# Even mixer: the division by the softmax sums on VectorE, and new tick counts for the normalised keys and the rotated queries

## The chip, the cores and the metric

The kernel runs on one core of one Trainium2 chip. The time is that of one execution on the device, in microseconds (us), and the median over the runs is compared. Engines are named as the profile names them: PE is TensorE's matmuls, PEld its weight loads, DVE is VectorE, ACT is ScalarE, POOL is GpSimd, SP is SyncE, whose queue issues the weight loads from HBM.

## The reference

A trunk of two layers on 256 tokens of width 1024, all in float32. Each layer is: half a SwiGLU block, a mixer, half a SwiGLU block. The mixer of layer 0, the "even" mixer, is the one the change touches:

```python
def even_mixer(h, w_in, q_gain, k_gain, sink, w_out, rope1, rope_axial):
    proj = h @ w_in                      # 1024 -> qa, ka, va, qb, kb, vb
    ...
    qa = apply_axial_rope(rms_norm(qa, q_gain), *rope_axial)   # 8 heads of 64
    ka = apply_axial_rope(rms_norm(ka, k_gain), *rope_axial)   # 2 key heads
    oa = global_gqa(qa, ka, va)
    qb = apply_rope(qb, *rope1)                                # 8 heads, plain
    kb = apply_rope(kb, *rope1)                                # 2 key heads
    ob = windowed_gqa_sink(qb, kb, vb, sink)
    return jnp.concatenate([oa, ob], axis=-1) @ w_out

# in both attentions
    p = jnp.exp(s - m)
    denom = jnp.sum(p, axis=-1)          # group b: + exp(sink - m)
    p = p / denom
    o = p @ v
```

Group "a" has normalised queries and keys and attends to all tokens; group "b" has plain ones, a window of 128 and a sink logit for each head. Layer 1 has another mixer ("odd"), which the change leaves alone.

## The kernel before

**Tiling.** Tokens are two tiles of 128 (`tt` 0 and 1). Weights come as pieces of 128 x 512. Each piece is split on the chip into a high part (`hi`, ACT, line 319) and the rest (`lo`, DVE, line 322), and each product takes three matmuls of 128x128 by 128x512: hi·hi, lo·hi and hi·lo (lines 311, 312, 313). Such a group of three is called a *triple* below. `th` and `tl` are the two parts of the transposed activations. Three of the eight PSUM banks are for keys' projections and attention scores (`s`), two for projections (`pj`), two for transposes (`tp`), one for attention outputs (`o`).

**Order.** PE, ACT, DVE and SP each execute their instructions in the order in which the program emits them. That order is set by *ticks*: each triple ends with one tick, and a tick steps every task (a Python generator) whose count has run out. `yield n` in a task means "go on n ticks later". So a number such as `ROPE_WAIT` is no time, but a count of triples that are emitted in between. A tick also may supply the next weight piece (`hi` at once, `lo` at the next tick). If nothing can be multiplied, ticks pass without a triple and the tasks' instructions stand close together.

**The even mixer's steps.** First the keys and values of both groups are projected (one bank `s` for each `tt`), then the queries of b, then those of a (banks `pj`). Four tasks `keys(g, tt)` evict, rotate (POOL, `rope`, lines 700 and 717), transpose on PE (`kr`, line 764) and split into `kT..z` (ACT) and `kT..x` (DVE, and a POOL copy, line 424). For group a they also normalise, by squares on ACT, a sum on DVE (`ssq`, line 728), a power on POOL (line 331) and a multiplication on POOL (line 759). Four tasks `queries(g, tt)` rotate on DVE (`t`, lines 700 and 702, `qr`, line 715), transpose on PE (line 394) and split into `qT..`, ACT's half and then DVE's.

The attention walks through group b, then group a, and in each through `tt`, then two pairs of heads (`b0`), then two halves `s`: eight *steps* for each group, numbered 1 to 8 below. A step is: scores on PE (lines 624, 625, and the mask, 628), maxima on DVE (`m`, 637), for b the sink (POOL, `es`, 573), exponentials with sums on ACT (`p`, 666; `es`, 577), `tot` and the reciprocal `r` on DVE (675, 678), the multiplication of `p` by `r` (680), four transposes on PE (688), their copy on ACT (`pt`, 584); after each second step the product with the values (`o`, 609) and its split `oT..h`, `oT..l`. A new step's scores start a fixed number of ticks after those before. The first step of a `tt` starts when the task of its queries has ended (`has_q`). Then `out_proj` multiplies by the output weights, for group b while group a's attention runs, then for group a, and adds to `x` (line 446).

The tick counts that the change touches stand at the top of the file:

```python
ROPE_WAIT = 3
KB_WAIT = 6
KA_WAITS = [2, 5]
```

Of the kernel before, what the change touches and what calls it, by code (L numbers as in the profile page):

```python
# [40 lines left out]
R_WAIT = 3  # L41
GLU_WAIT = 5
NAT_WAIT = 2
ROPE_WAIT = 3
KB_WAIT = 6
KA_WAITS = [2, 5]
QA_WAIT = 9
EVEN_GAP = {'a': 2, 'b': 2}
ODD_GAP = [4, 3]
# [73 lines left out]
class Trunk:  # L123
# [76 lines left out]
    def plan(self):  # L200
# [49 lines left out]

        yield from ffn("ffn1", 0, 0)
        yield from even()
        yield from ffn("ffn2", 0, 2)
        yield from ffn("ffn1", 1, 3)
# [476 lines left out]
    def even(self, sink):  # L731
        nc = self.nc
        self.rate = EVEN_RATE
        flat = lambda t: t.rearrange("p a b -> p (a b)")
        tab = {
            "a": [[self.gtab[:, tt, i, :] for i in range(4)] for tt in range(NT)],
            "b": [[self.tab[:, tt, i, :] for i in (4, 5, 2, 3)] for tt in range(NT)],
        }
        axial = {"a": 2, "b": 1}
        kT = {g: self.keys_tiles([P, T], f"kT{g}") for g in "ab"}  # L740
        vv = {g: [self.t([P, P], f"v{g}{tt}") for tt in range(NT)] for g in "ab"}
        qT = {g: [[], []] for g in "ab"}
        oT = {g: [[], []] for g in "ab"}
        by = [None, None]
        made = {"a": [], "b": []}

        def keys(g, tt, ps):
            yield 1
            r = self.rstd_of(tt)
            o = 256 if g == "b" else 0  # L750
            k = self.t([P, 2, HD], f"k{g}", 2)
            kr = self.t([P, 2, HD], f"kr{g}", 2)
            nc.scalar.activation(flat(k), ps[:, o : o + P], AF.Copy, scale=r)
            nc.scalar.activation(vv[g][tt], ps[:, o + P : o + 2 * P], AF.Copy, scale=r)
            if g == "a":
                sq = self.squares(k, 2, 1.0)
                yield KA_WAITS[0]
                n = self.head_rstd(sq, 2)
                nc.gpsimd.tensor_tensor(k, k, n.unsqueeze(2).to_broadcast([P, 2, HD]), op=ALU.mult)
                yield KA_WAITS[1]  # L760
            self.rope(nc.gpsimd, kr, k, 2, axial[g], *tab[g][tt][2:])
            yield KB_WAIT
            tb = self.bank("tp")
            nc.tensor.transpose(tb[:, :P], flat(kr), self.ident)
            yield 1
            at = slice(tt * P, tt * P + P)
            yield from self.stack_k(tb[:, :P], *([t[:, at] for t in tiles] for tiles in kT[g]))

        def queries(g, tt, ps):
            yield 1  # L770
            r = self.now.r[tt]
            x = ps.rearrange("p (a b) -> p a b", a=8)
            qr = self.t([P, 4, 2, HD], "qr", 2)
            if g == "a":

                sq = self.squares(x, 8, r)
                self.rope(nc.vector, qr, x, 8, axial[g], *tab[g][tt][:2])
                yield QA_WAIT
                n = self.head_rstd(sq, 8)
                by[tt] = self.little([P, 8], f"by{tt}")  # L780
                nc.gpsimd.tensor_scalar(by[tt], n, r, 1.0, op0=ALU.mult, op1=ALU.mult)
            else:
                self.rope(nc.vector, qr, x, 8, axial[g], *tab[g][tt][:2], r)
                yield ROPE_WAIT
            tb = self.turned(qr.rearrange("p j s d -> p (j s d)"))
            yield 1
            yield from self.stack_q(tb, f"qT{g}{tt}", 1, qT[g][tt])

        def heads(g):
            return self.attend(  # L790
                lambda tt: qT[g][tt],
                lambda tt: len(made[g]) > 2 + tt and all(task[1] is None for task in made[g][: 3 + tt]),
                lambda b: kT[g],
                lambda b, s, kc: vv[g][kc][:, s * HD : s * HD + HD],
                lambda: True,
                f"oT{g}",
                oT[g],
                EVEN_GAP[g],
                EVEN_WAITS[g],
                nc.gpsimd,  # L800
                sink=sink if g == "b" else None,
                scale=(lambda tt, b, s: by[tt][:, s * 4 + b : s * 4 + b + 2]) if g == "a" else None,
            )

        def both():
            yield from heads("b")
            yield from heads("a")


        W = self.take(KD)  # L810
        for tt in range(NT):
            ps = self.project(self.ready(tt), W, "s")
            for g in "ba":
                made[g].append(self.start(keys(g, tt, ps)))
        attention = None
        for g in "ba":
            W = self.take(KD)
            for tt in range(NT):
                ps = self.project(self.now.hT[tt], W, "pj")
                made[g].append(self.start(queries(g, tt, ps)))  # L820
                if attention is None:
                    attention = self.start(both())
        self.out_proj([oT["b"], oT["a"]], attention)
# [261 lines left out]
```

## Time and profile before

| what | before |
|---|---|
| median of 3 runs | 979.89 us (979.39 to 980.45) |
| the profiled execution's own time | 978.92 us |
| its span, first to last instruction | 977.1 us |
| PE busy | 965.5 us (99%) |
| DVE busy | 607.7 us (62%) |
| ACT busy | 546.0 us (56%) |
| POOL busy | 85.7 us (9%) |
| granted TensorE clock | 0.998 |

The even mixer takes about 200 us to 287 us of the span. Read the shares of the whole span with care: they average over blocks that have nothing in common. In the SwiGLU blocks PE runs without a gap; what the change can move is in the mixer, and there the row to look at is the idle time of PE and the instruction that ended it. A matmul's end is modelled, so the starts of consecutive matmuls tell more than the busy time.

### The profile page before, as it was taken

The page shows a single profiled execution, that of the slowest core. Times are in us where ns is not written, and L with a number is a line of the kernel's source. Part 1 is how long each engine was busy: PE and PEld are TensorE (multiplying, and loading weights), DVE is VectorE, ACT ScalarE, POOL GpSimd, SP SyncE. Part 2 cuts the span into 40 slices and gives each one's busy share as a digit, 9 for nine tenths or more (in the row PEclk, how much of TensorE's full clock was granted, in tenths as well). Part 3 has the DMA queues.
Part 4 walks back from the last instruction along what each step waited for, and adds up shares of the span by engine and source line. Part 5 has one row for each costly group of instructions (what it writes and reads, how often), then busy time and mean ns, then how long its engine had stood idle before and what let it go on. Part 6 is the DMA issues. An engine that isn't in the chain of part 4 may idle for free.

```text
span 977.1 us, 13724 instructions
## 1 busy us (share of the span) xinstructions
PE 965.5 (99%) x4908; PEld 818.6 (84%) x4908; DVE 607.7 (62%) x1195; ACT 546.0 (56%) x1152; POOL 85.7 (9%) x152
## 2 busy tenths in 40 slices
PE   9999999999999999999999999999999999999997
PEld 6888998877788889988888899888888888889886
DVE  6565575488866555654655566548879675555643
ACT  7544564477786544544644446447777664545430
POOL 0020000063420000000000000101331000000002
PEclk9999999999999999999999999999999999999999
DMA  8665576554226555766456456646545355547621
GB/s 290 223 205 172 182 251 214 168 135 120 96 91 208 176 157 158 246 215 197 148 176 197 145 173 231 223 153 197 181 128 170 130 172 181 186 131 235 237 87 43
DMA packets 82373, 171.70 MB, mean 176 GB/s; under 512 B 3712, under 2 KB 25216, under 8 KB 82304
## 3 DMA queue, kind: packets, MB, share of 16 engines
q1 hardware_dynamic: 81728, 170.23, 54.0%
q8 instruction: 38, 0.62, 0.3%
q10 hardware_dynamic: 576, 0.59, 0.2%
q14 instruction: 31, 0.25, 0.1%
HBM read 169.76 MB, written 1.05 MB: 175 GB/s over the span
## 4 chain that ended last, share of the span: by engine, by line
PE 95%; DVE 2%; ACT 1%; POOL 1%; issue 1%; DMA 0%; POOLq 0%; ACTq 0%
PE pj L311 14%; PE pj L313 14%; PE pj L312 14%; PE s L313 13%; PE s L312 13%; PE s L311 13%; PE tp L394 2%; PE o L311 2%; PE o L312 2%; PE o L313 2%; PE o L609 2%; PE tp L688 1%; PE tp L366 1%; PE s L624 1%; PE s L625 1%; DVE lo L322 1%
## 5 line engine op out<-in xcount | busy, mean ns | idle before, releaser
L322 DVE TENSOR_TENSOR lo<-raw,hi 128x512 fp32r<-128x512 f32 (+1 forms) x664 | 423.2, 671 | 239.1 <-ACT hi L319 235.0
L319 ACT ACTIVATE hi<-raw 128x512 fp32r<-128x512 f32 (+1 forms) x664 | 371.9, 606 | 169.4 <-PE s L313 102.4
L311 PE MATMUL pj<-hi,th 128*128 128x512 f32 (+1 forms) x512 | 197.8, 386 | 0.0
L313 PE MATMUL pj<-hi,tl 128*128 128x512 f32 (+1 forms) x512 | 192.8, 377 | 0.0
L312 PE MATMUL pj<-lo,th 128*128 128x512 f32 (+1 forms) x512 | 192.5, 376 | 0.0
L311 PE MATMUL s<-hi,th 128*128 128x512 f32 (+1 forms) x400 | 152.1, 380 | 0.0
L313 PE MATMUL s<-hi,tl 128*128 128x512 f32 (+1 forms) x400 | 149.2, 373 | 0.0
L312 PE MATMUL s<-lo,th 128*128 128x512 f32 (+1 forms) x400 | 148.9, 372 | 0.0
L313 PEld LDWEIGHTS pj<-hi,tl 128*128 128x128 f32 x512 | 96.1, 188 | 15.5
L311 PEld LDWEIGHTS pj<-hi,th 128*128 128x128 f32 x512 | 96.4, 188 | 13.0 <-issue 0.3
L312 PEld LDWEIGHTS pj<-lo,th 128*128 128x128 f32 x512 | 96.4, 188 | 12.8
L319 ACT ACTIVATE g_h<-tp 128x512 fp32r<-128x512 f32 (+1 forms) x48 | 27.0, 563 | 126.4 <-PE tp L394 126.4
L313 PEld LDWEIGHTS s<-hi,tl 128*128 128x128 f32 x400 | 75.2, 188 | 11.2
L312 PEld LDWEIGHTS s<-lo,th 128*128 128x128 f32 x400 | 75.3, 188 | 10.5 <-DVE lo L322 0.2
L311 PEld LDWEIGHTS s<-hi,th 128*128 128x128 f32 x400 | 75.3, 188 | 10.1
L313 PE MATMUL s<-hi,g_l 128*128 128x512 f32 (+2 forms) x198 | 73.6, 372 | 0.0
L312 PE MATMUL s<-lo,g_h 128*128 128x512 f32 (+2 forms) x198 | 73.5, 371 | 0.0
L311 PE MATMUL s<-hi,g_h 128*128 128x512 f32 (+2 forms) x198 | 73.5, 371 | 0.0
L505 DVE SCALAR_TENSOR_TENSOR glu<-pj,rstd,silu 128x512 f32<-128x512 f32 (+1 forms) x48 | 33.7, 702 | 45.1 <-PE pj L313 45.1
L500 ACT ACTIVATE silu<-s,rstd 128x512 f32<-128x512 f32 (+1 forms) x48 | 31.4, 654 | 51.1 <-PE s L313 50.6
L331 POOL TENSOR_TENSOR rstd<-var,mhalf 128x1 f32<-128x1 f32 (+2 forms) x16 | 12.9, 808 | 375.8 <-DVE var L329 375.8
L322 DVE TENSOR_TENSOR g_l<-tp,g_h 128x512 fp32r<-128x512 f32 (+1 forms) x48 | 30.8, 642 | 23.1 <-ACT g_h L319 23.1
(245 smaller groups left out, 1133.7 us busy)
## 6 DMA issues: line engine op xcount, KB each, us to landing
raw<-in_ffn_w_down SPq DMA_DIRECT2D x44, 1024.0 KB, 5.0
raw<-in_ffn_w_up SPq DMA_DIRECT2D x32, 1024.0 KB, 5.2
raw<-in_ffn_w_gate SPq DMA_DIRECT2D x30, 1024.0 KB, 5.1
raw<-in_ffn_w_gate SPq DMA_DIRECT2D x16, 768.0 KB, 4.4
raw<-in_ffn_w_up SPq DMA_DIRECT2D x16, 768.0 KB, 4.4
raw<-in_odd_w_qkv SPq DMA_DIRECT2D x12, 1024.0 KB, 5.2
raw<-in_even_w_in SPq DMA_DIRECT2D x4, 1024.0 KB, 5.1
raw<-in_even_w_out SPq DMA_DIRECT2D x8, 512.0 KB, 5.7
```

Source lines behind the costliest of these rows:

```text
L311: mm(ps, h, wh, start=first, stop=False)
L312: mm(ps, h, wl, start=False, stop=False)
L313: mm(ps, l, wh, start=False, stop=last)
L319: self.nc.scalar.activation(hi, src, AF.Copy)
L322: self.nc.vector.tensor_tensor(lo, src, hi.bitcast(F32), op=ALU.subtract)
L331: nc.gpsimd.tensor_tensor(r[:, :n], v[:, :n], self.mhalf[:, :n], op=ALU.pow)
L366: nc.tensor.transpose(tb[:, j * P : (j + 1) * P], self.x[tt][:, b * P : (b + 1) * P], self.ident)
L394: self.nc.tensor.transpose(tb[:, i * P : (i + 1) * P], src[:, i * P : (i + 1) * P], self.ident)
L500: nc.scalar.activation(s[:, :w], g[:, :w], AF.Silu, scale=self.rstd_of(tt))
L505: nc.vector.scalar_tensor_tensor(m[:, :w], u[:, :w], self.now.r[tt], s[:, :w], op0=ALU.mult, op1=ALU.mult)
L609: self.nc.tensor.matmul(O[64 * s : 64 * s + 64, i * P : i * P + P], v(b0 + i, s, kc), pT[s][:, i, kc, :], start=(kc == 0), stop=(kc == 1),)
L624: nc.tensor.matmul(S[:, i, :], q, kz[s], start=True, stop=False)
```

## The change

Four edits in the even mixer. The multiplication of the exponentials by the reciprocal sums (line 680) goes from POOL to DVE for both groups. The tasks of the normalised keys (group a) wait 8 ticks instead of 2 before their sum of squares, 4 instead of 5 before the rotation, and 10 instead of 6 before the transpose; the plain keys keep 6. The transposes of b's rotated queries come after 5 ticks instead of 3. And each query task ends two ticks later, so that the first scores of its `tt` can start only then.

```diff
-ROPE_WAIT = 3
-KB_WAIT = 6
-KA_WAITS = [2, 5]
+ROPE_WAIT = 5
+KB_WAIT = {'a': 10, 'b': 6}
+KA_WAITS = [8, 4]
...
-            yield KB_WAIT
+            yield KB_WAIT[g]
             tb = self.bank("tp")
             nc.tensor.transpose(tb[:, :P], flat(kr), self.ident)
...
             tb = self.turned(qr.rearrange("p j s d -> p (j s d)"))
             yield 1
             yield from self.stack_q(tb, f"qT{g}{tt}", 1, qT[g][tt])
+
+            yield 2
...
                 EVEN_GAP[g],
                 EVEN_WAITS[g],
-                nc.gpsimd,
+                nc.vector,
                 sink=sink if g == "b" else None,
```

How instructions move is shown at three places. In the listings a name carries the number of its buffer, and these numbers differ between the two kernels.

**Place 1, ACT, when group b's attention starts.** `qTb` from `tp_2474` (before) or `tp_2451` (after) is the split of b's second query tile; `p_2440` and `p_2465` are the exponentials of step 1, `p_2464` and `p_2493` those of step 2, and the table load stands ahead of the first exponential. Before:

```order
L319 ACTIVATE hi_2404<-raw_1891 128x512
L666 ACT_TABLE_LOAD
L666 ACTIVATE p_2440,sums_2367<-s_2369,m_637_2401 128x256 x2
L577 ACTIVATE es_2368<-es_2368 128x2
L319 ACTIVATE hi_2450<-raw_1891 128x512
L666 ACTIVATE p_2464,sums_2367<-s_2392,m_642_2414 128x256 x2
L577 ACTIVATE es_2368<-es_2368 128x2
L319 ACTIVATE qTb_662_2492<-tp_2474 64x512
L319 ACTIVATE qTb_663_2493<-tp_2474 64x512
```

After:

```order
L319 ACTIVATE hi_2435<-raw_1959 128x512
L319 ACTIVATE qTb_655_2461<-tp_2451 64x512
L319 ACTIVATE qTb_656_2462<-tp_2451 64x512
L666 ACT_TABLE_LOAD
L666 ACTIVATE p_2465,sums_2394<-s_2396,m_644_2422 128x256 x2
L577 ACTIVATE es_2395<-es_2395 128x2
L319 ACTIVATE hi_2475<-raw_1959 128x512
L319 ACTIVATE kTaz_524_2030<-tp_2459 64x128
L319 ACTIVATE kTaz_525_2031<-tp_2459 64x128
```

The split of the second query tile stood behind the exponentials of steps 1 and 2, and now stands ahead of the table load and of both. On PE its transposes (`tp_2451`) stand right behind the scores of step 3, one triple and the transpose of the second normalised key (`tp_2459`) follow, and after one more triple come the scores of step 4.

**Place 2, DVE, near the end of group b's attention.** `pj_2569` (before) and `pj_2508` (after) are a's second query tile, whose rotation is `t` and `qr`; `sums_2628` and `sums_2650` belong to steps 7 and 8. Before:

```order
L675 TENSOR_TENSOR tot_2736<-sums_2628,es_2629 128x2
L678 RECIPROCAL r_2738<-tot_2736 128x2
L675 TENSOR_TENSOR tot_2760<-sums_2628,es_2629 128x2
L678 RECIPROCAL r_2762<-tot_2760 128x2
L700 TENSOR_TENSOR t_8_741_2769<-pj_2569,gtab 128x512
L700 TENSOR_TENSOR t_8_742_2770<-pj_2569,gtab 128x8x16 x4
L715 TENSOR_TENSOR qr_2766<-t_8_741_2769,t_8_742_2770 128x4x64 x2
```

After:

```order
L700 TENSOR_TENSOR t_8_728_2720<-pj_2508,gtab 128x512
L700 TENSOR_TENSOR t_8_729_2721<-pj_2508,gtab 128x8x16 x4
L715 TENSOR_TENSOR qr_2717<-t_8_728_2720,t_8_729_2721 128x4x64 x2
...
L322 TENSOR_TENSOR qTa_740_2763<-tp_2745,qTa_740_2763 64x512
L322 TENSOR_TENSOR qTa_741_2764<-tp_2745,qTa_741_2764 64x512
L675 TENSOR_TENSOR tot_2789<-sums_2650,es_2651 128x2
L678 RECIPROCAL r_2791<-tot_2789 128x2
L680 TENSOR_SCALAR p_2785<-p_2785,r_2791 128x256 x2
L675 TENSOR_TENSOR tot_2811<-sums_2650,es_2651 128x2
L678 RECIPROCAL r_2813<-tot_2811 128x2
```

The reciprocals of steps 7 and 8 stood ahead of that rotation; now they stand behind it, behind the split of a's first query tile and, in the rows left out, behind two `lo`, `oTb02l`, the sums `ssq` and the maxima of step 8.

**Place 3, DVE, when group a's attention starts.** `qTa` here is the split of a's second query tile, and `s_2869`, `s_2887`, `s_2924` (before) and `s_2905`, `s_2922`, `s_2949` (after) are the scores of a's steps 1, 2, 3. Before:

```order
L637 TENSOR_REDUCE m_2905<-s_2869 128x2
L652 TENSOR_TENSOR m_781_2907<-m_2905,by_748_2791 128x2
L637 TENSOR_REDUCE m_2916<-s_2887 128x2
L652 TENSOR_TENSOR m_785_2918<-m_2916,by_748_2791 128x2
L322 TENSOR_TENSOR qTa_782_2912<-tp_2900,qTa_782_2912 64x512
L322 TENSOR_TENSOR qTa_783_2913<-tp_2900,qTa_783_2913 64x512
L322 TENSOR_TENSOR lo_2932<-raw_2184,hi_2931 128x512
L678 RECIPROCAL r_2941<-sums_2868 128x2
L678 RECIPROCAL r_2956<-sums_2868 128x2
L637 TENSOR_REDUCE m_2960<-s_2924 128x2
```

After:

```order
L322 TENSOR_TENSOR qTa_778_2897<-tp_2885,qTa_778_2897 64x512
L322 TENSOR_TENSOR lo_2913<-raw_2177,hi_2912 128x512
L637 TENSOR_REDUCE m_2927<-s_2905 128x2
...
L678 RECIPROCAL r_2963<-sums_2904 128x2
L680 TENSOR_SCALAR p_2960<-p_2960,r_2963 128x256 x2
L446 SCALAR_TENSOR_TENSOR x_86<-pj_2856,x_86 128x512
L678 RECIPROCAL r_2976<-sums_2904 128x2
L680 TENSOR_SCALAR p_2973<-p_2973,r_2976 128x256 x2
L637 TENSOR_REDUCE m_2980<-s_2949 128x2
```

The maxima of steps 1 and 2 stood ahead of the split of the second query tile and now stand behind it; between the reciprocals and the maxima of step 3 there are now two pairs of multiplications and an addition to `x`. On PE four triples that stood between the scores of a's steps 1 to 5 now stand earlier, and the scores of steps 3, 4 and 5 follow each other without a triple.

## The prediction

> **What bounds the kernel now.** I read the page first, then the idle time of PE by releaser, then PE, DVE and ACT in order of time through the mixer, last the share of each engine by stretch.
>
> ```profile
> PE 965.5 (99%) x4908; PEld 818.6 (84%) x4908; DVE 607.7 (62%) x1195; ACT 546.0 (56%) x1152; POOL 85.7 (9%) x152
> 220.00:230.00 10.00, 9.55 (x56) 7.76 (x56) 9.46 (x25) 7.00 (x19) 3.77 (x10) 1.00 0.56 128
> 250.00:260.00 10.00, 9.98 (x64) 8.07 (x63) 9.63 (x21) 4.76 (x10) 3.57 (x3) 1.00 0.33 108
> 260.00:270.00 10.00, 9.94 (x68) 7.79 (x67) 8.66 (x21) 8.96 (x28) 4.07 (x10) 1.00 0.34 105
> ```
>
> The first line is the span: PE bounds it, and DVE at 62% looks free. The others are stretches of the mixer; behind the length come PE, PEld, DVE, ACT and POOL. There DVE is busy 87 to 96%, nearly as long as PE. What is put on DVE here has little room, whatever the page's average says.
>
> ```profile
> 210.93 0.39 PE L312 MATMUL pj<-lo,th 128*128 128x512 f32 x1
> 211.16 0.39 PE L313 MATMUL pj<-hi,tl 128*128 128x512 f32 x1
> 212.40 0.33 PE L764 MATMUL tp<-mats,kra 128*128 128x128 f32 x1 [0.85 <-POOL kra L717]
> 217.37 0.63 PE L394 MATMUL tp<-mats,qr 128*128 128x128 f32 x4 [0.34 <-DVE qr L715]
> 220.18 0.39 PE L624 MATMUL s<-kTbz,qTb 128*128 128x256 f32 x1 [0.70 <-DVE qTb L322]
> ...
> 230.56 0.63 PE L688 MATMUL tp<-mats,p 128*128 128x128 f32 x4 [0.83 <-ACT pt L584]
> ...
> 249.40 0.47 PE L311 MATMUL pj<-hi,oTb00h 128*128 128x512 f32 x1 [0.75 <-DVE t L700]
> ```
>
> Start, duration, what, and in brackets PE's idle time and what ended it. Matmuls start 0.23 us apart (a triple is 0.69), so after 211.16 the next could start at 211.39 and started at 212.40: an idle time of 0.85 stands for 1.01 lost, 0.16 more than shown. So the five waits lose 1.01, 0.50, 0.86, 0.99 and about 0.9. They are what the mixer can give back, 4.3 us or 0.4%.
>
> **The change part by part.** *Normalised keys later.* Their rotation on POOL leaves the path of the plain keys, and their transposes stand 14 triples later: the wait at 212.40 goes. *Transposes of queries, and first scores, later.* Five ticks cover the rotation and four more triples stand ahead of the first scores, so the waits at 217.37 and 220.18 go. Together 2.37 gained. POOL has its chain done: before, the second plain key waited there behind the first normalised one; SP's loads keep their order. What is late next is worked out along the chain.
>
> *Step A, to the transposes of b's second query tile.*
>
> ```profile
> 223.18 1.28 ACT L666 ACT_TABLE_LOAD   x1 [2.04 <-DVE m L659]
> 224.47 0.47 ACT L666 ACTIVATE p<-s,m 128x256 f32<-128x256 f32 x1
> 225.39 0.20 ACT L577 ACTIVATE es<-es 128x2 f32<-128x2 f32 x1
> 226.63 0.28 PE L624 MATMUL s<-kTbz,qTb 128*128 128x256 f32 x1
> 227.30 0.61 PE L394 MATMUL tp<-mats,qr 128*128 128x128 f32 x4
> 227.94 1.20 ACT L319 ACTIVATE qTb<-tp 64x512 fp32r<-64x512 f32 x2 [0.83 <-PE tp L394]
> ```
>
> Before, PE reached them at 227.30. Now two more triples stand ahead of them (1.37), one group of scores less (0.67, from 226.63 to 227.30), one key transpose less (0.1) and no stall: 227.30 + 1.37 - 0.67 - 0.1 - 2.37 = 225.5.
>
> *Step B, place 1.* The split of this tile now stands ahead of the table load on ACT. It starts 0.64 behind the transposes and takes 1.20: 227.3. Table load and step 1's exponentials last from 223.18 to 225.39, and `es` to 225.59: done at 229.6 and 229.8. But the scores of step 4 need the bank of step 1's scores, the third of three. PE has two triples and five transposes in front of them and is there at 227.4: 2.1 lost. Then step 1's transposes need one of the two `tp` banks; one holds the second queries until DVE has split them, the other the late normalised key, whose split stands on DVE further behind. DVE: step 1's division from 229.8 (0.9), a `lo` 0.6, the split 1.4, so 232.7, and PE is there at 231.1: 1.7 lost. Step 2's wait for the copy that frees the same bank: 0.3. Sum 4.1, where before had 3.36 up to the same work: 0.7 slower so far.
>
> *Step C, the division on DVE.*
>
> ```profile
> L680 POOL TENSOR_SCALAR p<-p,r x32: 471/478/1023, 227.2 to 277.4; 128x256 f32<-128x256 f32 x32
> L680 DVE TENSOR_SCALAR p<-p,r x32: 344/351/355, 694.7 to 761.9; 128x256 f32<-128x256 f32 x32
> ...
> 697.46 0.17 DVE L678 RECIPROCAL r<-sums 128x2 f32<-128x2 f32 x1 [0.57 <-ACT p L666]
> 697.66 0.62 DVE L680 TENSOR_SCALAR p<-p,r 128x256 f32<-128x256 f32 x2
> 698.19 0.42 DVE L642 CUSTOM_DVE_ANT_1 p<-s,bias 128x256 f32<-128x256 f32 x1
> ```
>
> The odd mixer divides on DVE already: 0.35 against 0.48 on POOL for one, and a pair holds DVE for 0.53. That is 16 pairs, 8.5 us more on DVE in about 60 us, 4.3 of it in group b. By busy time that alone brings DVE from 95% of 220 to 230 to more than all.
>
> ```profile
> 222.21 0.69 DVE L637 TENSOR_REDUCE m<-s 128x2 f32<-128x512 f32 x1
> ...
> 223.02 0.69 DVE L322 TENSOR_TENSOR lo<-raw,hi 128x512 fp32r<-128x512 f32 x1
> ...
> 247.78 1.48 DVE L700 TENSOR_TENSOR t<-pj,gtab 128x512 f32<-128x512 f32 x5
> ...
> 249.97 0.69 DVE L322 TENSOR_TENSOR lo<-raw,hi 128x512 fp32r<-128x512 f32 x1
> 250.57 0.68 DVE L728 TENSOR_REDUCE ssq<-sq 128x8 f32<-128x512 f32 x1
> 251.36 0.42 DVE L322 TENSOR_TENSOR oTb10l<-o,oTb10h 128x256 fp32r<-128x256 f32 x1
> 251.70 0.68 DVE L322 TENSOR_TENSOR lo<-raw,hi 128x512 fp32r<-128x512 f32 x1
> 252.41 1.41 DVE L322 TENSOR_TENSOR qTa<-tp,qTa 64x512 fp32r<-64x512 f32 x2
> 252.30 1.09 PE L609 MATMUL o<-pt,vb 128*64 128x128 f32 x16
> ```
>
> From start to start: maxima with the sink 0.81, a rotation 2.19, `lo` 0.60, sums of squares 0.79, `oT` 0.34, a query split 1.41; `tot` with `r` and `p` 0.92 (0.19 + 0.20 + 0.53). By place 2 the rotation of a's second queries now stands ahead of steps 7 and 8, because it follows the projection, and the attention slid behind it. From 229.8 to the `p` of step 7 DVE has six such divisions (5.5), seven `lo` (4.2), six maxima (4.9), two rotations (4.4), query splits (2.8), a key split (0.6 as estimate from its four-row size), two `oT` (0.7), one sum of squares (0.8), one wait of 1.1 for step 6's `es` and 0.9 for step 7's own: 25.9, so step 7's transposes start at 255.7. PE's work in this stretch is 14 triples (9.7), five groups of scores (3.4), three output products (3.3) and seven groups of transposes (3.5 with restarts): 20. DVE, not PE, sets the pace.
>
> *Step D, to the last query split.*
>
> ```profile
> 257.84 0.60 PE L394 MATMUL tp<-mats,qr 128*128 128x128 f32 x4
> 258.48 1.19 ACT L319 ACTIVATE qTa<-tp 64x512 fp32r<-64x512 f32 x2 [3.61 <-PE tp L394]
> 260.35 0.56 ACT L666 ACTIVATE p<-s,m,by 128x256 f32<-128x256 f32 x1
> 263.87 0.56 ACT L666 ACTIVATE p<-s,m,by 128x256 f32<-128x256 f32 x1 [0.18 <-DVE m L652]
> 264.97 1.07 ACT L584 ACTIVATE pt<-tp 128x512 f32<-128x512 f32 x2
> ...
> 275.83 0.58 ACT L666 ACTIVATE p<-s,m,by 128x256 f32<-128x256 f32 x1
> 278.45 1.04 PE L688 MATMUL tp<-mats,p 128*128 128x128 f32 x8
> ```
>
> From 255.7 PE has four triples (2.8), steps 7 and 8 (0.9), an output product (1.1), restarts and a wait for a `pj` bank that an addition to `x` frees (0.5): transposes of a's last queries at 261.0, before 257.84.
>
> *Step E, place 3.* ACT's split 0.64 behind that and 1.19 long, then DVE's 1.41, a `lo` 0.6, maxima of step 1 with the scale 0.9: its exponentials start at 265.9, 4.9 behind the transposes, where before it was 2.5 (257.84 to 260.35), because the maxima stood ahead of the split. Then two pairs of divisions and an `x` stand ahead of step 3's maxima. From 265.0 DVE has maxima, `lo`, maxima, `x`, `lo`, division, `x`, division, maxima (0.9, 0.6, 0.9, 0.6, 0.6, 0.7, 0.6, 0.7, 0.9): step 3's exponentials at 271.5, before 263.87. Two exponentials take 1.1 (263.87 to 264.97), two copies 0.95: step 4's end at 274.7, before 267.0.
>
> *Step F.* The remaining steps are a loop over ACT, DVE and PE; each pair of steps gets one division (0.5) more between exponentials and the next maxima: 10.4 us instead of 9.4, so the last exponentials end at 285.1 instead of 276.4. PE's transposes of step 7, which stand some work behind in both, are at 286.7 instead of 278.45. From there both orders are alike.
>
> **Sum:** 286.7 - 278.45 = 8.2 slower. The profiled execution took 978.92 (span 977.1 and 1.8 around it), which gives 987.1; the median of the runs is 979.89, 1.0 above it, which gives 988.1. Costed at nothing: the later normalised keys, which only group a's scores read, some 30 us later; without that cover the 1.01 of 212.40 would come back.
>
> **A page against a row.** The next table load on ACT, behind the mixer:
>
> ```profile
> 293.53 0.68 ACT L319 ACTIVATE hi<-raw 128x512 fp32r<-128x512 f32 x1
> 294.23 1.28 ACT L500 ACT_TABLE_LOAD   x1
> ```
>
> The activation ends at 294.21 and the load starts at 294.23. The Trainium skill, "ScalarE: Activation LUTs", section "What ACT_TABLE_LOAD costs", has 1283 ns for the load, as here, and a drain of about 1380 ns besides. By that step B would be 1.4 longer and the result 989.5; this trace shows no drain, so I leave it out.
>
> **The rivals.**
>
> *Faster.* The attention keeps up: the waits go and nothing takes their place, 979.89 - 2.4 to - 4.3, about 976.5. For it: the division is 0.13 shorter, and three waits do go. Against it: step 1's exponentials would have to end by 227.4, so ACT's table load to start by 225.1, and its order has it behind a split that starts at 226.1. The Trainium skill, "GPSIMD Engine Reference", section 4.1, sends elementwise work to VectorE rather than GpSimd and so leans this way.
>
> *Same.* Place 1 costs what the front gains (+0.7), and DVE catches up later: 980.6. It takes DVE's 25.9 in step C down to PE's 20, a fifth off each instruction. For that speaks that POOL at work stretches some of them (the longest POOL `p` of 1.02 beside its 0.48 shows that the two disturb each other).
>
> *Slower by less.* Step C holds, step E does not: group a's attention waits no more than before, and only the 3.2 of step D stay (261.0 against 257.84): 983.1. It decides whether DVE has caught up when a's first scores are there.
>
> *Slower by more.* The load has a drain after all, or the divisions cost what they do on POOL (16 x 0.26 more): 989.5 to 992.
>
> **How the numbers follow.** My sum 0.53 (985 to 991), slower by less 0.20, same 0.10, faster 0.12, slower by more 0.05. A change under 0.2% (2 us) is about what a measurement of this kernel can't tell from none; so faster 0.12, same 0.10, slower 0.78. The range leaves out "faster", half of "same" and the top: 980.8 to 991.
>
> **What would show it.** Right: no idle PE ahead of line 764, the first `qr` and the first `qTb`; about 2 us ahead of step 4's scores released by ACT `p`; then waits of PE's line 688 for DVE, the largest in step 7; DVE over 95% from 230 to 257; PE idle time in the mixer near 12 us in place of 4. Wrong: step 1's exponentials done before PE wants the bank, or DVE idle where I have it full.

## The result, and the profile after

| | before | after |
|---|---|---|
| median | 979.89 us (979.39 to 980.45) | 989.35 us (989.05 to 990.86) |
| ratio, with its 95% interval | | 1.0097 (1.0084 to 1.0111) |
| the profiled execution, its span | 978.92, 977.1 us | 989.12, 987.3 us |

The change makes the kernel 9.5 us slower. (Of e4 and of the first run of f1 below only the times are used, since their profiled executions ran at a mean granted clock of 0.85 and 0.66.) The page's line of busy time:

```profile
PE 969.4 (98%) x4908; PEld 821.8 (83%) x4908; DVE 616.1 (62%) x1227; ACT 546.7 (55%) x1152; POOL 68.4 (7%) x120
```

The three stretches of the mixer that stand above for the kernel before (behind the length PE, PEld, DVE, ACT, POOL):

```profile
220.00:230.00 10.00, 7.88 (x47) 6.24 (x45) 7.67 (x18) 5.23 (x12) 1.44 (x5) 1.00 0.76 172
250.00:260.00 10.00, 7.14 (x46) 5.17 (x46) 9.58 (x28) 6.91 (x20) 2.07 (x3) 1.00 0.33 106
260.00:270.00 10.00, 9.61 (x60) 7.70 (x60) 8.04 (x16) 5.11 (x12) 1.92 (x2) 1.00 0.20 57
```

DVE has 8.4 us more and POOL 17.3 us less, as the moved division says. PE lost 2.1 and 2.9 us in the first two stretches, where before it lost 0.5 and nothing. PE in order of time, the rows that answer to those of before, and the new waits:

```profile
212.20 0.27 PE L764 MATMUL tp<-mats,krb 128*128 128x128 f32 x1
217.23 0.63 PE L394 MATMUL tp<-mats,qr 128*128 128x128 f32 x4
220.58 0.31 PE L624 MATMUL s<-kTbz,qTb 128*128 128x256 f32 x1
225.48 0.61 PE L394 MATMUL tp<-mats,qr 128*128 128x128 f32 x4
229.70 0.39 PE L624 MATMUL s<-kTbz,qTb 128*128 128x256 f32 x1 [2.12 <-ACT p L666]
233.02 1.09 PE L688 MATMUL tp<-mats,p 128*128 128x128 f32 x4 [0.97 <-DVE qTb L322]
251.09 0.47 PE L311 MATMUL pj<-hi,oTb00h 128*128 128x512 f32 x1 [1.70 <-DVE t L700]
257.28 0.63 PE L688 MATMUL tp<-mats,p 128*128 128x128 f32 x4 [1.51 <-DVE p L680]
...
262.81 0.60 PE L394 MATMUL tp<-mats,qr 128*128 128x128 f32 x4
270.84 0.39 PE L624 MATMUL s<-kTaz,qTa 128*128 128x256 f32 x1 [0.97 <-ACT p L666]
...
274.60 0.39 PE L624 MATMUL s<-kTaz,qTa 128*128 128x256 f32 x1 [1.63 <-ACT p L666]
288.71 1.03 PE L688 MATMUL tp<-mats,p 128*128 128x128 f32 x8
```

The first three rows carry no bracket: the stalls of the front are gone. In their place stand 2.12 and 0.97 at place 1, 1.70 (0.75 before) and 1.51 at place 2, 0.97 and 1.63 at place 3. The last transposes start at 288.71 where before they started at 278.45.

### The profile page after: what moved, and what is told of

It reads as the page before. It is cut to its first block, busy times and chain, and to the rows that moved or that the text cites. A ratio compares the mean times of both kernels' runs of the same rounds, so it can differ in the third digit from the quotient of the medians.

```text
span 987.3 us, 13701 instructions
## 1 busy us (share of the span) xinstructions
PE 969.4 (98%) x4908; PEld 821.8 (83%) x4908; DVE 616.1 (62%) x1227; ACT 546.7 (55%) x1152; POOL 68.4 (7%) x120
## 4 chain that ended last, share of the span: by engine, by line
PE 94%; DVE 3%; ACT 1%; issue 0%; DMA 0%; POOL 0%; POOLq 0%; ACTq 0%; DVEq 0%
PE pj L311 14%; PE pj L313 14%; PE pj L312 14%; PE s L313 13%; PE s L312 13%; PE s L311 12%; PE tp L394 2%; PE o L311 2%; PE o L312 2%; PE o L313 2%; PE o L609 2%; PE tp L688 1%; DVE lo L322 1%; PE tp L366 1%; PE s L624 1%; PE s L625 1%
## 5 line engine op out<-in xcount | busy, mean ns | idle before, releaser
L500 ACT ACTIVATE silu<-s,rstd 128x512 f32<-128x512 f32 (+1 forms) x48 | 31.4, 654 | 51.1 <-PE s L313 50.7
L312 PEld LDWEIGHTS s<-lo,g_h 128*128 128x128 f32 x198 | 37.2, 188 | 6.7
```

The source lines that it names most:

```text
L312: mm(ps, h, wl, start=False, stop=False)
L500: nc.scalar.activation(s[:, :w], g[:, :w], AF.Silu, scale=self.rstd_of(tt))
```

## The experiments

Theory when they were designed: the later queries make group b late, and DVE, filled by the division, cannot catch up; both are needed. Rivals: the division alone; the order alone; and, once the trace was there, PE's clock, which halves twice in the mixer.

One measure is used throughout. The start of the program differs by up to 2.3 us between executions (the first transpose of `krb` stands between 206.5 and 208.8), so positions in the mixer are counted from that transpose. Against the kernel before, triples that the order has moved ahead of a position (0.69 each), and transposes of queries moved ahead of it (0.45: from 262.81, two triples later comes 264.63), are taken off. What is left is time lost up to there. Stretch 1 ends with b's scores of step 6, stretch 2 with a's first scores, stretch 3 with the last transposes of `p`. Each row comes from one profiled execution and is rounded so that it adds up; the sums lie within 0.8 us of the medians.

| kernel | stretch 1 | 2 | 3 | sum (trace) | median against before |
|---|---|---|---|---|---|
| changed | 2.7 | 3.1 | 4.3 | 10.1 | +9.5 |
| e1, division alone | 0.6 | 0.2 | 2.0 | 2.8 | +2.2 |
| e2, order alone | 3.0 | 4.3 | 2.4 | 9.7 | +9.6 |
| e3, keys alone | 0.3 | 0.4 | 0.4 | 1.1 | +0.7 |
| f1, transposes later | 1.0 | 2.9 | 2.2 | 6.1 | +6.1 |
| f2, first scores later | 1.8 | 2.9 | 1.7 | 6.4 | +7.2 |
| g2, changed, with fillers | 0.9 | 3.8 | 4.4 | 9.1 | +9.0 |
| h1, changed, table load early | -0.3 | 3.7 | 4.4 | 7.8 | +8.1 |
| h0, before, table load early | 0.0 | 0.0 | 0.0 | 0.0 | +0.3 |

Worked for the changed kernel at the end of stretch 1: scores of step 6 at 240.65, less 206.62, is 34.03; before 235.06 less 206.50 is 28.56; 5.47 less four triples (2.74) is 2.7. In f1 the row is that of the second execution.

**e1, the division alone.**

```diff
                 EVEN_WAITS[g],
-                nc.gpsimd,
+                nc.vector,
```

> Only the division of the even mixer moves from POOL to DVE; the order stays as before. My theory (the late order makes group b late, and the fuller DVE then cannot catch up: both are needed for the whole loss): the three stalls of the front (2.37 in sum) stay, step 1's exponentials stand early as before, so only the DVE chain of step C grows: 982 to 986 us. Rival 'the division alone does it': 988 or more. Rival 'the order alone does it': 980.5 or less.

Measured: 982.27 us, ratio 1.0024 (1.0014 to 1.0034). Of PE's waits that are not in the kernel before, or are longer there, the three largest, in time order:

```profile
251.65 0.47 PE L311 MATMUL pj<-hi,oTb00h 128*128 128x512 f32 x1 [1.13 <-DVE t L700]
267.97 0.39 PE L624 MATMUL s<-kTaz,qTa 128*128 128x256 f32 x1 [0.88 <-ACT p L666]
273.33 0.50 PE L313 MATMUL pj<-hi,oTa00l 128*128 128x512 f32 x1 [1.08 <-DVE oTa00l L322]
```

The size falls in the range of "both are needed", but not at its place: group b's part loses 0.8, group a's 2.0, at waits for ACT and DVE. "The division alone" (988 or more) falls.

**e2, the order alone.** The changed kernel with the division given back to POOL.

```diff
                 EVEN_WAITS[g],
-                nc.vector,
+                nc.gpsimd,
```

> The order of the change (normalised keys, transposes of queries and first scores later), with the division left on POOL. My theory: PE waits about 2 us ahead of step 4's scores as in the changed kernel, its granted clock falls behind it, but DVE's chain to step 7 is some 3.7 us shorter and group a's steps are about 1 us shorter: 981.5 to 985 us. Rival 'the order alone does it': 987 to 989.5. Rival 'the division alone does it': the three stalls of the front go and nothing comes back, 978 or less.

Measured: 989.69 us, ratio 1.0097 (1.0083 to 1.0111): as slow as the changed kernel. My theory falls; the rival "the order alone" was right (its range ended at 989.5; the four executions lie between 987.71 and 990.25). PE in order of time:

```profile
230.96 0.39 PE L624 MATMUL s<-kTbz,qTb 128*128 128x256 f32 x1 [2.12 <-ACT p L666]
233.79 1.08 PE L688 MATMUL tp<-mats,p 128*128 128x128 f32 x4 [1.14 <-POOL kTax L424]
251.90 0.47 PE L311 MATMUL pj<-hi,oTb00h 128*128 128x512 f32 x1 [1.03 <-DVE t L700]
258.35 0.44 PE L688 MATMUL tp<-mats,p 128*128 128x128 f32 x2 [1.78 <-POOL p L680]
```

Step 7's transposes (the last row) start 50.5 behind the first `krb`, in the changed kernel 50.7 (257.28 less 206.62). Six divisions fewer on DVE moved them by 0.2. What DVE waited for from 230 to 258, in the changed kernel and then in e2 (us in total, times, longest):

```profile
DVE tot L675 <- ACT es L577: 1.7, 2, 1.4
DVE lo L322 <- ACT hi L319: 0.2, 1, 0.2
```

```profile
DVE tot L675 <- ACT es L577: 4.5, 3, 2.1
DVE lo L322 <- ACT hi L319: 2.5, 3, 1.5
```

The two stretches do not hold quite the same work: step 1's `tot` waits 2.1 us for ACT in both kernels, but in the changed one it starts at 229.77, just ahead of the stretch, and in e2 at 231.03, inside it. Over the same work DVE waits 4.0 us in the changed kernel and 7.0 us in e2. Freed of six divisions (3.2 us), DVE waits 3.0 us longer for ACT and finishes no earlier. Why step 7 is late all the same, DVE and POOL in e2:

```profile
250.27 1.48 DVE L700 TENSOR_TENSOR t<-pj,gtab 128x512 f32<-128x512 f32 x5
251.78 0.76 DVE L715 TENSOR_TENSOR qr<-t,t 128x256 f32<-128x256 f32 x2
...
254.36 1.65 POOL L331 TENSOR_TENSOR rstd<-var,mhalf 128x8 f32<-128x8 f32 x1 [3.57 <-DVE var L329]
255.77 1.39 DVE L322 TENSOR_TENSOR qTa<-tp,qTa 64x512 fp32r<-64x512 f32 x2
257.19 0.16 DVE L675 TENSOR_TENSOR tot<-sums,es 128x2 f32<-128x2 f32 x1
257.81 2.27 POOL L680 TENSOR_SCALAR p<-p,r 128x256 f32<-128x256 f32 x4 [1.39 <-DVE tot L675]
```

`rstd` on POOL is the power for a's first queries. The rotation of a's second queries and the split of its first stand ahead of `tot` of step 7, as the order of place 2 has it. DVE executes in order, so `tot` stands behind them whether the division follows on DVE or on POOL. POOL itself is ready before: it waits 1.39 us for DVE.

**e3, the keys alone.**

```diff
-KB_WAIT = 6
-KA_WAITS = [2, 5]
+KB_WAIT = {'a': 10, 'b': 6}
+KA_WAITS = [8, 4]
...
-            yield KB_WAIT
+            yield KB_WAIT[g]
```

> Of the change only the later chain of the normalised keys. My theory: the stall of 1.01 at the first normalised key's transpose goes, nothing is late behind it since group a reads these keys some 30 us later: 978 to 979.5 us. Rival 'a later order costs by itself' (a tp bank held longer by the late keys): 980.5 or more.

Measured: 980.81 us, ratio 1.0009 (1.0 to 1.0017); the gain of 1.01 that I expected is not there, and the rival's 980.5 or more is met, though the interval just touches no change. The wait at the normalised key is gone, and the next one has taken it over:

```profile
218.09 0.63 PE L394 MATMUL tp<-mats,qr 128*128 128x128 f32 x4 [1.34 <-DVE qr L715]
```

Before it was 0.34 there. PE arrives 1.0 earlier and waits 1.0 longer for the same rotation; the `tp` bank that the rival named is not what ends this wait. A stall at the front is a time by which a chain is not ready, and taking one cause away shows the next.

**e4, the queries alone**, both edits:

```diff
-ROPE_WAIT = 3
+ROPE_WAIT = 5
...
             yield from self.stack_q(tb, f"qT{g}{tt}", 1, qT[g][tt])
+
+            yield 2
```

> Of the change only the later transposes of rotated queries and the later first scores; keys and division as before. My theory: stalls of 0.50 and 0.86 at the front go, but the split of b's second queries stands ahead of the table load on ACT, so PE waits about 2 us ahead of step 4's scores and loses clock behind it: 982 to 985 us. Rival 'place 1 costs no more than the front gains': 978.5 to 980.5.

Measured: 988.62 us, ratio 1.0090 (1.0076 to 1.0103). Nearly the whole loss; more than I expected, because I looked for it at place 1 only. So each of the two edits was run by itself.

**f1, only the transposes later** (`ROPE_WAIT = 5`), run twice, and **f2, only the first scores later** (`yield 2`).

> The kernel before with the transposes of rotated queries later alone (five ticks), without the two ticks behind a query split; keys and division as before. ACT has the table load and step 1's exponentials ahead of b's second query split, as before. Theory 'place 1 decides' (the second split ahead of the table load makes PE wait about 2 us for step 4's scores, and PE's granted clock halves behind it): none of that here, and the stalls of 0.50 and 0.86 shrink: 978 to 981.5 us. Rival 'later queries cost wherever they stand' (the rotation of a's second queries ahead of the attention on DVE, group a's first scores later): 984 or more.

> The same kernel as in f1_rope_only, for a usable trace: 985.3 to 987 us. Theory 'the lost cover': scores start two triples later against the projections, so the rotation of a's second queries comes onto DVE ahead of the last steps of group b, and PE's idle time sits from step 5 of group b on. Rival 'place 1': at least 3 us of idle time or lost clock up to step 6's scores of group b.

> The kernel before with the two ticks behind a query split alone (first scores two triples later); the rest as before. On ACT the table load and the first exponentials of step 1 stand ahead of b's second query split, step 2's behind. Theory 'place 1 decides': PE waits less than 1.5 us ahead of step 4's scores and keeps its clock: 979 to 983 us. Rival 'later scores cost wherever they stand': 984 or more.

Measured: f1 986.17 us, ratio 1.0064 (1.0050 to 1.0078), and again 985.92 us, 1.0068 (1.0052 to 1.0083); f2 987.11 us, 1.0074 (1.0061 to 1.0086). In f1 ACT has the table load and step 1's exponentials ahead of b's second query split, as before, and loses only 1.0 up to step 6's scores. "Place 1 decides" falls, "later queries cost wherever they stand" was right. The stalls of the front, which I had expected to shrink, are still in f1's trace (0.87, 0.52 and 0.79 us of idle time); f2's keeps 0.85 and 0.34. f1's largest waits of PE behind place 1:

```profile
250.26 0.47 PE L311 MATMUL pj<-hi,oTb00h 128*128 128x512 f32 x1 [1.22 <-DVE t L700]
254.57 0.90 PE L688 MATMUL tp<-mats,p 128*128 128x128 f32 x4 [1.46 <-POOL p L680]
268.85 0.38 PE L624 MATMUL s<-kTaz,qTa 128*128 128x256 f32 x1 [0.99 <-ACT p L666]
271.38 0.39 PE L624 MATMUL s<-kTaz,qTa 128*128 128x256 f32 x1 [0.86 <-ACT p L666]
```

These are places 2 and 3 again, with the division on POOL and with two triples moved instead of four. Here DVE has the reciprocals of step 7 and 8 done at 252.97, and POOL brings the wait itself:

```profile
252.39 1.65 POOL L331 TENSOR_TENSOR rstd<-var,mhalf 128x8 f32<-128x8 f32 x1 [3.39 <-DVE tot L675]
254.03 1.40 POOL L680 TENSOR_SCALAR p<-p,r 128x256 f32<-128x256 f32 x3
```

Before, the power and the split of a's first query tile stood behind the divisions of steps 7 and 8. In f1 the power (1.65, on POOL) stands ahead of them, and PE waits for POOL; the split (1.39, on DVE) still follows the reciprocals, at 253.59. With the whole order of the change, as in e2, the split stands ahead too, and DVE's `tot` comes last. As far as these rows show, that is why the engine of the division made no difference at place 2.

**g1 and g2, the clock.** In the trace of the changed kernel PE is granted half its clock twice (the column behind POOL's busy time):

```profile
227.00:230.40 3.40, 1.28 (x8) 0.76 (x7) 1.24 (x5) 3.38 (x9) 0.62 (x1) 1.00 0.96 230
230.50:237.20 6.70, 5.72 (x19) 4.32 (x18) 6.43 (x19) 3.94 (x12) 1.41 (x4) 0.50 0.17 35
237.40:240.00 2.60, 2.60 (x27) 1.93 (x26) 2.50 (x10) 2.03 (x10) 0.00 (x0) 1.00 0.02 6
271.40:274.80 3.40, 1.44 (x11) 0.99 (x10) 2.73 (x10) 1.45 (x5) 0.00 (x0) 1.00 0.01 2
274.90:278.20 3.30, 3.30 (x23) 2.74 (x23) 1.91 (x7) 2.10 (x7) 0.00 (x0) 0.50 0.00 0
```

Ten us at half clock are 5 us of PE's work, half of the loss by that count. To tell whether they lie on the path, matmuls that nobody reads were put into the idle places, so that PE stays busy while the waits stay:

```diff
+            fill = {(True, 0, 2, 1): 13, (False, 1, 0, 0): 6, (False, 1, 0, 1): 10}
+            for _ in range(fill.get((sink is not None, tt, b0, s), 0) if norm is nc.vector and gap == 2 else 0):
+                nc.tensor.matmul(self.bank("o")[:, : 3 * P], self.ident16, self.m16[:, : 3 * P], start=True, stop=True)
             S = self.scores(tt, b0, s, qT(tt), kT, sink is not None)
...
+        self.m16 = m16
```

These are g1's counts; g2 has 5, 2 and 4 in place of 13, 6 and 10.

> The changed kernel with products on PE whose result nobody reads (bf16, 384 columns, 0.16 us each, into the free output bank) at three places where PE idles: 13 ahead of step 4's scores (idle 2.12), 6 and 10 ahead of the fifth and sixth scores of group a (idle 0.97 and 1.63). They leave the waits as they are and take the idle time away. Theory 'half of the loss is PE's clock, which halves after an idle stretch' (0.50 for 6.8 and 3.4 us, 5.1 us of PE's work): no stretch at 0.50, 983 to 986 us. Rival 'the clock is not on the path, DVE and ACT set the pace there': 988.5 to 990.

> The changed kernel with products whose result nobody reads, at the same three places as before, but 5, 2 and 4 of them in place of 13, 6 and 10, since one took 0.36 us there (13 from 228.39 to 233.06) and not 0.16: 1.8, 0.7 and 1.4 us in idle stretches of 2.12, 0.97 and 1.96. Theory 'the clock is on the path': no stretch at 0.50; what the first trial gave back (it took 10.5 us of products into 5 us of idle time and was no slower) stays as a gain: 984 to 987 us. Rival 'the clock is hidden behind DVE and ACT': 988.5 to 989.7.

Measured: g1 989.74 us, ratio 1.0098 (1.0084 to 1.0112); inconclusive by itself, since its matmuls took 0.36 each, more than twice the 0.16 that I had reckoned, and filled more than the idle time. g2, with fewer: 988.75 us, 1.0093 (1.0080 to 1.0107). The same two stretches in g2, then its PE waits at place 1:

```profile
230.50:237.20 6.70, 4.72 (x27) 3.28 (x27) 5.66 (x16) 5.22 (x18) 1.23 (x3) 1.00 0.39 81
274.90:278.20 3.30, 3.19 (x30) 2.70 (x31) 1.90 (x7) 2.50 (x8) 0.00 (x0) 1.00 0.00 0
```

```profile
231.16 0.39 PE L627 MATMUL s<-kTbz,qTb 128*128 128x256 f32 x1 [0.42 <-ACT p L669]
234.40 0.66 PE L691 MATMUL tp<-mats,p 128*128 128x128 f32 x4 [1.56 <-DVE qTb L322]
```

The clock is full, and the time is within 1 us of the changed kernel's (0.6 between the medians, 1.0 between the sums of the table). PE's faster matmuls only wait longer: 1.56 for `qTb` at step 1's transposes instead of 0.97. The rival was right: in these places half a clock costs about a tenth of the loss at most; the intervals of the two ratios overlap.

It need not be so cheap everywhere. f1's executions with a mean granted clock of 0.999 took 985.28 to 985.50 us, those with 0.998 took 985.95 to 986.34, and those with 0.997 took 987.32 and 987.56. Of some 984 us, 0.002 are 2.0 us of PE's work, and about that much is in the time. f1's usable trace is of an execution with 0.999, so it stays open where the others lose it, and whether the clock is the cause there or a sign of longer waits.

**h1 and h0, the table load early.** An exponential of a constant column, issued behind step 1's first scores:

```diff
             S = self.scores(tt, b0, s, qT(tt), kT, sink is not None)
+            if sink is not None and (tt, b0, s) == (0, 0, 0):
+                early = self.little([P, 1], "early")
+                nc.scalar.activation(early, self.mhalf[:, 0:1], AF.Exp)
```

> The changed kernel with one exponential of a constant column issued on ACT right behind step 1's first scores, so that the table load runs in ACT's idle time ahead of b's second query split. Theory 'place 1 decides': step 1's exponentials end 1.28 earlier, PE waits 0.8 instead of 2.1 ahead of step 4's scores and keeps its clock there: 983 to 986.5 us. Rival 'the wait alone counts, not the clock': 988. Rival 'DVE sets the pace behind it': 989 to 989.7.

> As h1_early_load, but the early exponential writes into a column that the kernel has already, not into a new one. If the new column, which moves the tiles behind it, made the matmuls of the feed-forward's last product 3% longer (0.2335 against 0.2267 us from start to start): back to 0.2267 there, and 987 to 988.5 us, since the mixer itself was 2.1 us shorter than in the changed kernel. If it was the exponential: 991.8 again.

Measured: h1_early_load 991.80 us, ratio 1.0122 (1.0106 to 1.0137); h1_no_new_tile, which writes into the existing column "warm" instead, 987.87 us, 1.0083 (1.0069 to 1.0096). The groups of the feed-forward's last product (140 to 180 us, ahead of the mixer), first with the new column, then without (count, busy, mean ns):

```profile
L313 PE MATMUL s<-hi,g_l 128*128 128x512 f32 x29 | 11.5, 395 | 0.0
```

```profile
L313 PE MATMUL s<-hi,g_l 128*128 128x512 f32 x29 | 11.3, 389 | 0.0
```

So the 991.8 was the new column's doing and says nothing of the load; the second run answers the question. With the load early, place 1 loses nothing any more (-0.3 in place of 2.7), and about 1.5 us of the 9.5 come back (the four executions lie between 986.98 and 988.67). The rest stays in stretches 2 and 3.

> The kernel before with the table load run early, in ACT's idle time ahead of step 1's maxima, through an exponential of a constant column into a column that is there already. If step 1's exponentials set the wait of 0.99 at its transposes (230.56): 978 to 979.3 us, faster than before. If that wait has another cause (the copy of step 1's transposes, released by PE): 979.5 to 980.5.

Measured on the kernel before: 980.06 us, ratio 1.0005 (0.9996 to 1.0013). The wait at step 1's transposes went from 0.83 to 0.51 of idle time, which no median shows. No version that was run beats the kernel before.

## Why the prediction was right in its number, and wrong in its main reason

It said 988.1 (980.8 to 991) and slower; measured 989.35.

- **Front and step A: right.** The three stalls are gone, and b's second transposes start at 225.48 (predicted 225.5).
- **Step B: right, with one omission.** Scores of step 4 wait 2.12 (predicted 2.1) for step 1's exponentials, at 229.70 (229.6); step 1's transposes start at 233.02 (232.8). ACT in order of time:

```profile
226.13 1.20 ACT L319 ACTIVATE qTb<-tp 64x512 fp32r<-64x512 f32 x2 [4.74 <-PE tp L394]
227.33 1.28 ACT L666 ACT_TABLE_LOAD   x1
228.62 0.47 ACT L666 ACTIVATE p<-s,m 128x256 f32<-128x256 f32 x1
```

  The load starts as the split ends, so the drain of which the Trainium skill ("ScalarE: Activation LUTs", "What ACT_TABLE_LOAD costs") speaks doesn't show here either; leaving it out was right. What I left out wrongly is the clock, which halved right behind that wait; it made this stretch lose 2.7 net where I had 0.7. With the clock kept (g2) it was 0.9, but most of the difference was lost again behind it, 0.7 of it in stretch 2.
- **Step C: the failed step.** The time was near (step 7's transposes at 257.28, predicted 255.7), the reason wrong. "DVE, not PE, sets the pace" was read from a sum of 25.9 us on DVE, in which six divisions count 3.2 (six times 0.53). Without them (e2) DVE waits 3.0 us longer over the same work, and step 7 is 0.2 earlier. Nor was DVE as full in the changed kernel as I had said: it was busy for 23.98 of the 27 us from 230 to 257, 89% and not over 95%, and less in the middle of that stretch (PE, PEld, DVE, ACT, POOL):

```profile
240.00:250.00 10.00, 9.39 (x68) 7.56 (x68) 7.70 (x23) 7.09 (x20) 1.00 (x3) 1.00 0.34 105
```

  The chain goes through ACT, PE and DVE in turn, and the rotation that has come ahead of steps 7 and 8 delays it. A nearly full engine beside a fixed order is not yet the cause. The mechanism in words (attention slid behind the rotation) stood in the prediction, the price was put on the wrong term. Priced so, the order without the division should have taken 981.5 to 985 us, and it took 989.69; that the whole sum still came out near is in part luck.
- **Step D: near in size.** a's last query transposes at 262.81, 5.0 later than before; predicted 3.2 later. Of the 1.8 between, 1.6 are there already at the end of step C (257.28 against 255.7).
- **Steps E and F: right in size, half right in reason.** The last transposes are 10.3 late (predicted 8.2); from the transposes of a's last queries to them it took 25.9 us (predicted 25.7). Of stretch 3's 4.3, the order alone brings 2.4 (e2), and the division 1.9 more; it gives 1.2 back in stretch 2. By itself on the old order the division costs 2.2 us, on the new order nothing that the medians show (989.35 against 989.69).
- **The rivals.** "Faster" fell with the waits that came. "Same" fell: behind place 1 stretches 2 and 3 lost another 7.4 us, and nothing was caught up even where DVE had idle time (e2). "Slower by less" had group a's attention wait no more than before; stretch 3 lost 4.3. "Slower by more" lies nearest in time, but its drain and its dearer divisions are not in the trace. The rival that I hadn't: the order alone. The two causes don't add: 2.2 and 9.6 separately, 9.5 together.

What stays open: no run undid the rotation's place at place 2 alone, so that it is the cause there is read from the order on DVE and POOL in three traces (changed, e2, f1), and not shown by its removal.

## What to carry to other kernels

Where work is emitted in a fixed order, moving the start of a latency chain behind more filler can take that filler away from the chain's end. Here two triples (1.4 us) moved ahead of the first scores cost 6 to 7 us net (f1, f2) and left most of the front's stalls where they were; the whole new order removed all 2.4 us of them and still cost 9.6 (e2). Don't price a move by the busy time of the fullest engine; undo the suspected term alone before you believe the sum, because a sum can come out right with the wrong term in it. And when an experiment adds a tile, look at stages that it can't concern: here one column cost 4 us.

## What the runs showed of the hardware that I had not expected

- **Half clock after short waits.** The granted clock fell to 0.50 for 6.7 us and 3.3 us (rows above) though no idle stretch of PE was longer than 2.12 us. In the 3.4 us ahead of each, PE was busy 1.28 and 1.44 of 3.40. The Trainium skill, "TensorE: Matmul & The Clock Gate", part 1, has windows of 3.413 us that run freely, and half the clock after an idle one; the two lengths, about two windows and one, agree with that. It warns of idle gaps over about 3.4 us; here a window that was some 60% idle was enough.
- **Matmuls into one bank.** 128x384 bf16 products that each start anew in the same PSUM bank followed each other every 0.36 us at full clock (13 in 4.67 us in g1). Whether the shared bank is the reason was not tried.
- **A tile's place.** One new column of four bytes for each partition, in a pool that other stages share, made the matmuls of the feed-forward's last product 395 ns instead of 389 long and their starts 0.233 instead of 0.227 apart; the kernel took 3.9 us more (991.80 against 987.87). Which address does it wasn't tried.
